# A seven-product block multiplication for the input projection of a streaming encoder layer

## The chip, the cores and the metric

The kernel runs on one core of a Trainium2 chip. A core has a matrix engine, TensorE (PE in the profile, with its weight loads as PEld), and three engines for elementwise work: VectorE (DVE), ScalarE (ACT) and GpSimd (POOL). SyncE (SP) issues the transfers between HBM and the on-chip memory SBUF; matmul results land in PSUM. The metric is the device time in microseconds.

## The reference

One layer of an encoder is computed for 2048 prompt tokens and 64 sample tokens, all in float32. The input is row-normalised and multiplied by one wide matrix, and the columns of the product feed two branches:

```python
h = rmsnorm(x, norm_g) @ w_in                     # (tokens, 1024) @ (1024, 6144)
qa, ka, va, za, qb, kb, vb, zb, ga, gb = jnp.split(h, _split_points(), axis=-1)
```

Branch A is differential attention (q and k row-normalised per 64 columns, a chunk mask, the difference of two softmaxes, times v); the sample also attends to 4096 cached keys. Branch B is chunkwise retention with a running state. Each branch is normalised, gated by silu(z) and projected; sigmoid gates merge the two, and a last projection with a residual gives y. The outputs are y, the new k and v, and the retention states.

## The kernel before

Every float32 product that needs precision is made of three matmuls in the format that the profile calls fp32r: an operand is cast (high part), the cast is subtracted from the original (low part), and high x high, high x low and low x high are summed in PSUM.

The input projection runs over two halves of the tokens. `w_load` brings W in pieces of 256 KB, `w_piece` casts each on ACT (L470), and `w_low` subtracts on POOL (L480; three early pieces on DVE, L477). This is done for both halves, 192 pieces in all. `mm_group` (L516) goes through the eight 128-row slices of the inner dimension and issues a trio of matmuls for each. For v, k, q and the retention's v the tokens are stationary and 512 or 256 columns of W move (`natural`; the output lies with tokens on partitions). For the rest W is stationary and 512, 320 or 256 tokens move (`transposed`). The rows of x are normalised and turned by PE transposes (`x_tile`, L385); q and k are normalised with a row sum (L680) and turned as well (L707). `opening` orders the first token tile by hand.

All results go to scratch tensors in DRAM. A second stream of work, `z_stream`, reads them back for attention (`qk_block`, `softmax`, `at_pv`), the cached sample attention and the retention blocks; the third, `out_stream`, makes the two branch projections (`m_tile`, L1685 to L1687) and the output projection (`y_tile`, L1758 to L1760).

The order on PE, ACT and DVE is fixed when the program is built: each stream is a generator, and a planner, `loop`, always advances the most urgent one whose operands and buffers are ready by its own estimate of durations. On the chip each engine then takes its instructions strictly in that order, and waits where something is late. Buffers are counted by name in `BUFS`: "mm" are the PSUM banks of the projection, "w" the split pieces of W. DMAs are all issued by SP, in order.

## Time and profile before

| | |
|---|---|
| runs | median 1970.54 us of 3 (1969.14 to 1971.57) |
| profiled execution, span | 1970.5 us |
| granted PE clock, mean | 0.998 |
| busy: PE, DVE, ACT, POOL | 99%, 53%, 50%, 21% |
| projection matmuls at L516, three groups each of 1280 and 824 | 1363 us and 765 us busy |
| DMA | 286 MB, 145 GB/s on average |

A row of groups names line, engine, operation, output and inputs with their shapes, the count, then the busy time, the mean duration of one in ns and the idle time before it with what ended it. Matmuls overlap in the pipeline, so the busy times of L516 add up to more than the span; for PE the distance between the starts of two matmuls says what one costs. In a row of waits stand the total, the number of times and the longest, in us. A row of the timeline begins with start and duration in us; a row on one line gives the shortest, median and longest duration in ns.

### The profile page before, as it was taken

To read this page: it belongs to the slowest core of one execution; us is meant where nothing else is said; L and a number is where in the kernel's file an instruction comes from. 1 tells how busy PE (TensorE), PEld (TensorE's weight loads), DVE (VectorE), ACT (ScalarE), POOL (GpSimd) and SP (SyncE) were. 2 spreads that over 40 slices of the span, in tenths; PEclk is the share of its full clock that TensorE was granted. 3 is DMA by queue.
4 is the path that set the end of the run, shared out by engine and by line. 5 is a ranking of instruction groups with operands and counts; after the bars stand their busy time and mean duration, and the time that the engine had idled before them with its cause. 6 is when DMAs were issued, how large, how long until landed. Compare 5 with 4: busy or idle time off the path is not lost. (4 is left out here: it accounts for less than half of the span.)

```text
span 1970.5 us, 34013 instructions
## 1 busy us (share of the span) xinstructions
PE 1954.8 (99%) x12158; PEld 1753.9 (89%) x12158; DVE 1048.8 (53%) x2795; ACT 993.2 (50%) x2190; POOL 418.9 (21%) x387
## 2 busy tenths in 40 slices
PE   9999999999999999999999999999999999999999
PEld 7878999999988989999998888888888888888997
DVE  6553665536555236547757656635753356444433
ACT  6432776655544436436756666635654554333321
POOL 2310211212111121212112112112112434222210
PEclk9999999999999999999999999999999999999999
DMA  7647554336655656664352342553234666444432
GB/s 245 212 129 195 152 158 122 110 89 164 180 162 166 163 158 194 189 198 148 105 144 92 97 134 78 160 148 97 65 94 130 197 215 205 145 134 136 140 94 60
DMA packets 332429, 286.03 MB, mean 145 GB/s; under 512 B 65250, under 2 KB 296930, under 8 KB 332259
## 3 DMA queue, kind: packets, MB, share of 16 engines
q1 hardware_dynamic: 332258, 283.85, 49.0%
q8 instruction: 96, 1.57, 0.4%
q14 instruction: 75, 0.61, 0.1%
HBM read 187.22 MB, written 91.49 MB: 141 GB/s over the span
## 5 line engine op out<-in xcount | busy, mean ns | idle before, releaser
L516 PE MATMUL mm<-xh,wh 128*128 128x512 f32 (+2 forms) x1280 | 459.1, 359 | 0.0
L516 PE MATMUL mm<-xh,wl 128*128 128x512 f32 (+2 forms) x1280 | 452.3, 353 | 0.0
L516 PE MATMUL mm<-xl,wh 128*128 128x512 f32 (+2 forms) x1280 | 451.7, 353 | 0.0
L480 POOL TENSOR_TENSOR wl<-ws,wh 128x512 fp32r<-128x512 f32 x189 | 257.0, 1372 | 814.9 <-ACT wh L470 629.5
L516 PEld LDWEIGHTS mm<-xh,wl 128*128 128x128 f32 x1280 | 241.0, 188 | 31.6
L516 PEld LDWEIGHTS mm<-xh,wh 128*128 128x128 f32 x1280 | 241.3, 189 | 29.0 <-issue 0.2
L516 PEld LDWEIGHTS mm<-xl,wh 128*128 128x128 f32 x1280 | 241.6, 189 | 27.9
L516 PE MATMUL mm<-wh,xh 128*128 128x256 f32 (+1 forms) x824 | 258.4, 314 | 1.2 <-DVE tlo L753 1.0
L516 PE MATMUL mm<-wh,xl 128*128 128x256 f32 (+1 forms) x824 | 253.4, 308 | 0.0
L516 PE MATMUL mm<-wl,xh 128*128 128x256 f32 (+1 forms) x824 | 253.1, 307 | 0.1
L1119 DVE TENSOR_TENSOR atl<-at,ath 128x512 fp32r<-128x512 f32 (+1 forms) x144 | 93.8, 660 | 162.6 <-ACT ath L1117 162.6
L810 ACT COPY ev<-mm 128x512 f32<-128x512 f32 x140 | 71.5, 511 | 194.1 <-PE mm L516 166.0
L516 PEld LDWEIGHTS mm<-wh,xh 128*128 128x128 f32 x824 | 156.7, 190 | 10.9 <-DVE tlo L753 1.4
L516 PEld LDWEIGHTS mm<-wl,xh 128*128 128x128 f32 x824 | 156.9, 190 | 9.2 <-POOL wl L480 0.3
L516 PEld LDWEIGHTS mm<-wh,xl 128*128 128x128 f32 x824 | 156.7, 190 | 8.0
L1035 ACT ACTIVATE row<-row,a_mx 128x1024 f32<-128x1024 f32 (+7 forms) x160 | 153.9, 963 | 12.9 <-DVE a_mx L1015 12.6
L1005 DVE CUSTOM_DVE_ANT_0 row<-s,dfar 128x512 f32<-128x512 f32 (+2 forms) x192 | 118.6, 631 | 54.5 <-PE s L997 54.0
L470 ACT CAST wh<-ws 128x512 fp32r<-128x512 f32 x192 | 116.2, 619 | 44.8 <-PE mm L516 18.5
L1117 ACT CAST ath<-at 128x512 fp32r<-128x512 f32 (+1 forms) x144 | 79.0, 564 | 104.8 <-PE at L1104 97.4
L996 PE MATMUL s<-K,q 128*128 128x512 f32 (+3 forms) x320 | 118.7, 374 | 1.4 <-DVE a_acc L1005 1.4
L997 PE MATMUL s<-K,q 128*128 128x512 f32 (+3 forms) x320 | 115.2, 363 | 0.4 <-DMA q<-qT 0.4
L1057 DVE SCALAR_TENSOR_TENSOR row<-row,a_w 128x1024 f32<-128x1024 f32 (+4 forms) x96 | 103.6, 1086 | 14.4 <-ACT row L1054 14.1
(238 smaller groups left out, 4036.1 us busy)
## 6 DMA issues: line engine op xcount, KB each, us to landing
ws<-in_w_in_dram SPq DMA_DIRECT2D x192, 256.0 KB, 3.0
q<-qT SPq DMA_DIRECT2D x128, 128.0 KB, 3.1
V<-vN SPq DMA_DIRECT2D x24, 512.0 KB, 5.5
K<-kT SPq DMA_DIRECT2D x48, 256.0 KB, 4.2
gt<-gaT SPq DMA_DIRECT2D x64, 132.0 KB, 2.1
gt<-gbT SPq DMA_DIRECT2D x64, 132.0 KB, 2.2
xt<-in_x_prompt_dram SPq DMA_DIRECT2D x16, 512.0 KB, 6.1
kn<-in_cache_k_T_dram SPq DMA_DIRECT2D x32, 256.0 KB, 3.7
```

What stands on the lines that cost most here:

```text
L470: self.nc.scalar.copy(h, st)
L480: self.nc.gpsimd.tensor_sub(l, st, h.bitcast(F32))
L516: nc.tensor.matmul(ps, p, q, start=c == 0 and i == 0, stop=c == KC - 1 and i == 2)
L810: nc.scalar.copy(ev, ps)
L996: nc.tensor.matmul(ps, q1s, kk, start=True, stop=False)
L997: nc.tensor.matmul(ps, q2s, kk, start=False, stop=True)
L1005: nc.vector.tensor_tensor_reduce(out=units[k0 // 1024][:, k0 % 1024:k0 % 1024 + n], in0=ps, in1=tab, scale=-SLOPES[h], scalar=3.0e38, op0= ...
L1035: nc.scalar.activation(u, u, AF.Exp, bias=mx, scale=-1.0, accum_out=lp[:, k:k + 1])
L1057: nc.vector.scalar_tensor_tensor(out=u0, in0=u0, scalar=w[:, 0:1], in1=u1, op0=ALU.mult, op1=ALU.add)
L1117: nc.scalar.copy(ah[:, :w], at[:, :w])
L1119: nc.vector.tensor_sub(al[:, :w], at[:, :w], ah[:, :w].bitcast(F32))
```

## The change

The tokens of each of three groups (two, three and three 256-token pairs; the first with the sample) are split into two halves of 288 or 384, the inner dimension into two halves of 512, and W into 24 blocks of 256 columns, each of two halves of 128. For such a 2x2 by 2x2 block product the usual eight block products become seven, P1 to P7 (Winograd's form of Strassen's scheme): four combinations of the x blocks, made once per group, four of the W blocks, made for every block and group, and sums of the products. In each product a W block (or combination) is stationary and 288 or 384 tokens move.

`x_half` normalises x (now read already turned, in a layout prepared by the host) and forms the combinations; those of later groups are stored to DRAM and fetched back (`x_fill`). `w_comp` forms the combinations of W (T1 to T4 in the wr buffers) and splits all seven into high and low parts (wc). Two helpers, `tt` and `cast`, place each of these operations on POOL or on DVE or ACT by the planner's clock. `proj` issues the products in the order P1, P6, P2, P5, P7, then P1 of the next block, P3, P4, three PSUM banks in turn; `evac` copies or adds the results. Everything now leaves the projection with channels on partitions, so v, k and the retention's v are turned by PE afterwards (`turned`, L1716; L894), while the transposes of x and q fall away, and the q and k norms use a matmul with a block-ones matrix (L1776). V is fetched per pair of key tiles, the pools of the output stage open when the projection's close, and attention runs over three token groups instead of two halves.

```diff
-ROWS = 10
-BUFS = {"thi": 1, "tlo": 2, "ev": 3, "q": 2, "K": 4, "V": 4, "ath": 2, "atl": 2,
-        "ws": 3, "w": 12, "r_o": 1, "r_sq": 1, "r_y": 1, "r_hi": 1, "r_lo": 1, "state": 2,
-        "mm": 2, "s": 2, "at": 2, "pv": 1, "tp": 1,
+ROWS = 9
+BUFS = {"ev": 5, "t5": 6, "q": 2, "K": 4, "V": 3, "ath": 2, "atl": 2, "wc": 5, "wr": 7, "state": 1, "xs": 4,
+        "mm": 3, "s": 2, "at": 2, "pv": 1,
         "oz": 11, "og": 16, "gt": 8, "wst": 4, "m": 16, "xt": 2, "yt": 2}
 LAT = 250.0
...
+GROUPS = [(0, 2, 32), (2, 3, 0), (5, 3, 0)]
+
+ORDER = ["P1", "P6", "P2", "P5", "P7", "P3", "P4"]
+NCP = 24
...
-    def mm_group(self, ps, n, us, wsl, x, wfirst, last, between=None):
-        nc = self.nc
-        seg, xsl = x
-        if ps.shape[0] == 64:
-            both = self.both
...
-            ops = ((a, xh), (a, xl), (b, xh)) if wfirst else ((xh, a), (xh, b), (xl, a))
...
-            for i, (p, q) in enumerate(ops):
-                nc.tensor.matmul(ps, p, q, start=c == 0 and i == 0, stop=c == KC - 1 and i == 2)
-                self.P(n)
...
+    def tt(self, op, out, a, b, n, ready, pool=None):
+
+        if pool is None:
+            pool = max(self.pool, ready) + 2.6 * n < max(self.dve, ready) + 1.25 * n + (BIAS[max(0, self.turned_w) // NCP] if self.xcount[0] == 2 else 0.0)
+        eng = self.nc.gpsimd if pool else self.nc.vector
+        getattr(eng, "tensor_" + op)(out, a, b)
+        return (self.G if pool else self.V)(n, ready)
+
+    def cast(self, out, a, n, ready):
+        if max(self.pool, ready) + 1.35 * n + 50 < max(self.act, ready) + 0.84 * n + 165 + CBIAS:
+            self.nc.gpsimd.tensor_copy(out, a)
+            self.pool = max(self.pool, ready) + 1.35 * n + 50
+            return self.pool + LAT
+        self.nc.scalar.copy(out, a)
+        return self.A(n, ready)
...
+    def x_half(self, g, u, got, rx, pre):
...
+        a21, t21 = yield from self.x_stage(g, u, 1, 0, "K")
+        a22, t22 = yield from self.x_stage(g, u, 1, 1, "K")
+        t21 = yield from norm(1, 0, a21, t21)
+        t22 = yield from norm(1, 1, a22, t22)
+        ts1 = self.tt("add", s1, a21, a22, 2 * n, t22)
+        ts3 = self.tt("sub", a21, a11, a21, 2 * n, ts1)
+        t = max(t11, ts1, ts3)
+        if t > self.pe:
+            yield t - LAT
+        ts2 = self.tt("sub", a11, s1, a11, 2 * n, t)
+        t = max(t12, ts2)
+        if t > self.pe:
+            yield t - LAT
+        ts4 = self.tt("sub", a12, a12, a11, 2 * n, t)
+        for j, x, t in ((1, a11, ts4), (3, s1, ts2), (4, a21, ts3), (5, a12, ts4), (6, a22, ts1)):
+            self.give("K" if j in (4, 6) else "row", (yield from split(j, x, t)))
...
+    def w_comp(self):
+        nc = self.nc
+        for n in range(3 * NCP):
+            yield lambda: len(self.wq) > 0 and len(self.wq[0]) == 5
+            (b11, t11), (b12, t12), (b21, t21), (b22, t22), (b3, _) = self.wq.pop(0)
+
+            def split(k, r, t, last=True):
+                yield from self.take("wc")
+                w = self.sb(self.wp, [128, 2, 4, 128], "wc", dt=F32R)
+                if t > self.pe:
+                    yield t - LAT
+                t = self.cast(w[:, 0], r, 512, t)
+                yield t
+                t = self.tt("sub", w[:, 1], r, w[:, 0].bitcast(F32), 512, t)
+                self.wch[n, k] = (w, t)
+                if last:
+                    self.give("wr", t)
+                return t
+
+            t1 = yield from split("P1", b11, t11, False)
+            self.turned_w = n
+            yield max(t12, t1 - LAT)
+            t1 = self.tt("sub", b11, b12, b11, 512, t1)
+            yield t22
+            t2 = self.tt("sub", b3, b22, b11, 512, t1)
+            t3 = self.tt("sub", b12, b22, b12, 512, t1)
+            yield from split("P6", b3, t2, False)
+            t4 = yield from split("P2", b21, t21, False)
+            t4 = max(t4, t2)
+            yield t4 - LAT
+            t4 = self.tt("sub", b21, b21, b3, 512, t4)
+            self.give("wr", t4)
+            for k, w, t in (("P5", b11, t2), ("P7", b12, t3), ("P3", b22, t22), ("P4", b21, t4)):
+                yield from split(k, w, t)
+
+    def proj(self):
+        seq = []
+        for n in range(3 * NCP):
+            first, last = n % NCP == 0, n % NCP == NCP - 1
+            seq += [(n, "P1")] if first else []
+            seq += [(n, "P6"), (n, "P2"), (n, "P5"), (n, "P7")]
+            seq += [] if last else [(n + 1, "P1")]
+            seq += [(n, "P3"), (n, "P4")]
+        bank = {"P1": "a", "P6": "a", "P7": "a", "P4": "a", "P2": "b", "P5": "c", "P3": "c"}
+        after = {"P6": "T", "P7": "U2", "P4": "C22", "P3": "V"}
+        nc = self.nc
+        st = {}
+        for n, k in seq:
+            g, j = n // NCP, ORDER.index(k)
+            nn = cols(g)
+            p0, np_, s = GROUPS[g]
+            if k == "P1":
+                st[n] = {}
+            q = st[n]
+            b = bank[k]
+            if b not in q:
+                yield from self.take("mm")
+                q[b] = self.psum("mm")[:, :nn]
+            fresh = k in ("P1", "P2", "P5")
+            if k in after:
+                yield lambda: after[k] in q
+                if q[after[k]][1] > self.pe:
+                    yield q[after[k]][1]
+            yield lambda: len(self.xr.get((g, j), ())) == 2 and (n, k) in self.wch
+            w, t = self.wch.pop((n, k))
+            t = max(t, *self.xr[g, j])
+            if t > self.pe:
+                yield t
+            x = self.xt[g, j]
+            for c in range(4):
+                wh, wl, xh, xl = w[:, 0, c], w[:, 1, c], x[:, 0, c], x[:, 1, c]
+                for m, (u, v) in enumerate(((wh, xh), (wh, xl), (wl, xh))):
+                    nc.tensor.matmul(q[b], u, v, start=fresh and c == 0 and m == 0,
+                                     stop=c == 3 and m == 2, skip_group_check=True)
+                    t = self.P(nn)
+                if c == 1:
+                    yield self.pe
+            self.give("wc", t)
+            if n % NCP == NCP - 1:
+                self.xfree[g, j] = t
+            self.spawn(self.evac(n, k, q, t), 0, "w")
+            yield self.pe
+
+    def evac(self, n, k, q, t):
+        nc = self.nc
+        nn = cols(n // NCP)
+        if k in ("P1", "P6", "P5", "P4"):
+            yield from self.take("ev")
+            c = self.sb(self.ep, [128, 384], "ev", "ev")[:, :nn]
+            if t > self.pe:
+                yield t
+            nc.scalar.copy(c, q["c" if k == "P5" else "a"])
+            t = self.A(nn, t)
+            q[{"P1": "T", "P6": "U2", "P5": "V", "P4": "C21"}[k]] = (c, t)
+            if k == "P4":
+                self.give("mm", t)
+                self.finish(n, 0, 1, c, t)
+            return
+        b, src, ct, a = {"P2": ("b", "T", 0, 0), "P7": ("a", "V", 1, 1), "P3": ("c", "U2", 1, 0)}[k]
+        yield lambda: src in q
+        c, t2 = q[src]
+        t = max(t, t2)
+        if t > self.pe:
+            yield t
+        nc.vector.tensor_add(c, q[b], c)
+        t = self.V(nn, t)
+        if k == "P7":
+            q["C22"] = (c, t)
+        else:
+            self.give("mm", t)
+        self.finish(n, ct, a, c, t)
+
...
+        yield lambda: self.live["w"] == 0
+        self.z2.close()
+        self.z3 = self.es.enter_context(self.tc.tile_pool(name="p3a", bufs=1))
+        self.ms = self.z3.tile([128, 8, 2, 64], F32R, tag="ms", name="ms")
+        self.ogs = []
+        self.wout = []
+        self.spawn(self.out_prep(), 5)
+        yield lambda: len(self.wo[0]) == 4 and len(self.wo[1]) == 4
+        self.spawn(self.out_stream(), 8)```

The order of the instructions at three places. PE (the matrix engine), from its first real work. Before: the norm weights spread over the partitions (gz), transposes of x, then the projection, one 512-column matmul at a time (xh and xl are the high and low parts of x, wh those of W):

```order
L304 MATMUL s<-gz,ones 128x512 x2
L316 MATMUL at<-ones 128x128 x2
L385 MATMUL tp<-ident,xt 128x128 x4
L385 MATMUL pv<-ident,xt 128x128 x4
L574 MATMUL mm<-wh,xh_114 128x512
L574 MATMUL mm<-wh,xl_115 128x512
```

Now (dg spreads a row norm; x_195, x_299, x_204 and x_303 are the x operands of P1, P6, P2 and P5):

```order
L1628 MATMUL mm<-x_195,wc 128x288 x12
L1411 MATMUL s<-dg,ones 128x128 x2
L1409 MATMUL s<-dg,ones 128x32
L1628 MATMUL mm<-x_299,wc 128x288 x12
L1628 MATMUL mm<-x_204,wc 128x288 x12
L1628 MATMUL mm<-x_303,wc 128x288 x12
```

The transposes are gone, and the second product, P6, reads a combination of all four x blocks. DVE, where that combination is made (xa, xs and xR hold blocks and combinations, two half slices each; x_299 is the operand of P6):

```order
L1476 SCALAR_TENSOR_TENSOR xa<-xa,gT,xR 128x288 x4
L1353 TENSOR_TENSOR xR<-xa 128x576
L1353 TENSOR_TENSOR xa<-xa 128x576
L1353 TENSOR_TENSOR xa<-xR,xa 128x576
L1353 TENSOR_TENSOR x_299<-xa,x_299 128x576
L1353 TENSOR_TENSOR xa<-xa 128x576
L1353 TENSOR_TENSOR x_306<-xa,x_306 128x576
L1353 TENSOR_TENSOR x_313<-xa,x_313 128x576
L1353 TENSOR_TENSOR x_299<-xa,x_299 128x576
```

The second half of P6's operand is split after five other operations of the same kind. Before, DVE did two subtractions per x tile here (L393). POOL, the same stretch (wr are W blocks and combinations, wc their parts):

```order
L1353 TENSOR_TENSOR wc<-wr,wc 128x512
L1353 TENSOR_TENSOR wr<-wr 128x512 x2
L1358 CAST wc<-wr 128x512 x2
L1353 TENSOR_TENSOR wc<-wr,wc 128x512 x2
L1358 CAST x_204<-xa 128x576
L1353 TENSOR_TENSOR wc<-wr,wc 128x512
```

Before, POOL had a single row here, `L480 TENSOR_TENSOR wl<-ws,wh` thirteen times; now combinations, casts and parts of x stand between the parts of W.

At the end of the projection, PE now:

```order
L1628 MATMUL mm<-x_12793,wc 128x384 x6
L872 MATMUL s<-rqk 128x128 x4
L877 MATMUL at<-ident,rqk 128x128 x4
L894 MATMUL at<-ident,rru 128x128 x4
...
L956 MATMUL at<-ident,rru 128x128 x4
L1135 MATMUL mm<-ogh,w_o_diffh_20230 128x264
L1136 MATMUL mm<-ogl,w_o_diffh_20230 128x264
L1137 MATMUL mm<-ogh,w_o_diffl_20231 128x264
```

Between the last projection matmul and the first of the output stage stand only steps of two retention blocks (L872 to L956; the third follows among the first output matmuls). Before, a projection matmul (L516) stood directly ahead of L1685.

1311 lines of the change are left out of this document (562 added, 749 removed).

## The prediction

> **What bounds the kernel now.** I read the page's busy times and slices first, then what TensorE (PE) waited for, then the spacing of its matmuls.
>
> ```profile
> PE 1954.8 (99%) x12158; PEld 1753.9 (89%) x12158; DVE 1048.8 (53%) x2795; ACT 993.2 (50%) x2190; POOL 418.9 (21%) x387
> PE   9999999999999999999999999999999999999999
> POOL 2310211212111121212112112112112434222210
> PEclk9999999999999999999999999999999999999999
> q1 hardware_dynamic: 332258, 283.85, 49.0%
> ```
>
> PE is busy in all 40 slices at full granted clock; DVE and ACT are half idle, POOL four fifths. A busy PE is not a PE at its peak, so the waits come next.
>
> ```profile
> PE mm L574 <- ACT wh L470: 2.0, 2, 1.3
> PE s L996 <- DVE a_acc L1005: 1.4, 2, 0.8
> 17.80 0.48 PE L574 MATMUL mm<-wh,xh 128*128 128x512 f32 x1
> ```
>
> The largest wait of PE on any line is 2.0 us in the whole run; from 17.80 us on, the matmuls follow each other without a gap. So the time is the sum of PE's spacings, and PE work that is taken out comes off the end as long as the helpers deliver. How far apart matmuls of each width start (first and last row of a stretch of one width, from the timeline; a row gives start, duration, instruction):
>
> ```profile
> 1500.22 0.40 PE L516 MATMUL mm<-xl,wh 128*128 128x512 f32 x1
> ...
> 1503.89 0.39 PE L516 MATMUL mm<-xh,wl 128*128 128x512 f32 x1
> ...
> 401.01 0.31 PE L516 MATMUL mm<-xh,wh 128*128 128x320 f32 x1
> ...
> 401.88 0.39 PE L516 MATMUL mm<-xh,wh 128*128 128x512 f32 x1
> ...
> 301.85 0.28 PE L516 MATMUL mm<-xh,wh 128*128 128x256 f32 x1
> ...
> 302.55 0.28 PE L996 MATMUL s<-K,q 128*128 128x256 f32 x1
> ...
> 300.10 0.34 PE L996 MATMUL s<-K,q 128*128 128x384 f32 x1
> 300.28 0.34 PE L997 MATMUL s<-K,q 128*128 128x384 f32 x1
> ...
> 23.23 0.60 PE L385 MATMUL tp<-ident,xt 128*128 128x128 f32 x4
> 23.67 0.60 PE L385 MATMUL pv<-ident,xt 128*128 128x128 f32 x4
> ```
>
> 512 columns: 3.67 us over 16 starts, 0.229 us. 320: 0.87/6, 0.145. 256: 0.70/6, 0.117. 384: 0.18 from one pair, 0.173 on the line between 256 and 512; I take 0.175. 288, between 256 and 320: 0.132. A 128-column transpose: 0.44/4, 0.11.
>
> **The change, part by part.** First PE. The old projection by its forms (each row stands for a trio of equal counts):
>
> ```profile
> L516 PE MATMUL mm<-xh,wh 128*128 128x512 f32 x768 | 304.6, 397 | 0.0
> L516 PE MATMUL mm<-wh,xh 128*128 128x512 f32 x184 | 74.4, 404 | 0.2 <-ACT raw L672 0.2
> L574 PE MATMUL mm<-wh,xh 128*128 128x512 f32 x8 | 4.5, 556 | 2.0 <-ACT wh L470 2.0
> L516 PE MATMUL mm<-wh,xh 128*128 128x256 f32 x640 | 184.0, 288 | 1.0 <-DVE tlo L753 1.0
> L516 PE MATMUL mm<-xh,wh 128*128 128x256 f32 x256 | 73.7, 288 | 0.0
> L516 PE MATMUL mm<-xh,wh 128*128 128x320 f32 x256 | 80.8, 315 | 0.0
> L512 PE MATMUL mm<-wh,xs 128*128 128x512 f32 x24 | 9.4, 394 | 0.0
> L707 PE MATMUL tp<-ident,raw 128*128 128x128 f32 x128 | 19.3, 273 | 0.0
> ```
>
> 3 x 960 x 0.229 = 660 us, 3 x 896 x 0.117 = 314 us, 3 x 256 x 0.145 = 111 us, and some 15 us for the sample's tile (L512 and its sisters): 1100 us. The new one has 24 column blocks x 7 products x 12 matmuls in each of three token groups, 2016 of 288 columns and 4032 of 384: 2016 x 0.132 + 4032 x 0.175 = 266 + 706 = 972 us. **Saved: 128 us.** Transposes: the 136 of x (L385) and 136 of q and k (L707) go, 30 us; 144 of v and k (L1716, L1719) and 68 of the retention's v (L894) come, 23 us; so do 96 matmuls for the q and k norms (L1776, L1777), 15 us, and 18 that spread the row norms, 2 us. **Net +10 us.** The profiled execution's own time is its span, 1970.5 us, and the runs' median is 1970.54, so no correction is needed: with helpers that keep up, 1970.5 - 128 + 10 = 1852 us.
>
> Now the helpers, which is where the price lies. One pass is one column block for one token group; there are 72. Each needs 7 casts, 7 subtractions for low halves and 4 combinations of W, all 128x512: 504 casts and 792 tensor-tensor operations where 192 and 192 stood. The built program puts 669 of the 792 and 189 casts on POOL, 123 on DVE, 315 casts on ACT. Their prices, and what happens when DVE and POOL meet:
>
> ```profile
> L480 POOL TENSOR_TENSOR wl<-ws,wh x189: 1258/1296/2281, 10.2 to 1566.0; 128x512 fp32r<-128x512 f32 x189
> L398 POOL CAST xs<-xl 128x256 fp32r<-128x256 f32 x2 | 0.7, 402 | 0.0
> L470 ACT CAST wh<-ws 128x512 fp32r<-128x512 f32 x192 | 116.2, 619 | 44.8 <-PE mm L516 18.5 <-DMA ws<-in_w_in_dram 11.5 <-issue 9.7
> L1704 DVE TENSOR_TENSOR gt<-mm,gt 128x264 f32<-128x264 f32 x64 | 27.5, 429 | 30.0 <-PE mm L1687 30.0
> L1119 DVE TENSOR_TENSOR atl<-at,ath 128x512 fp32r<-128x512 f32 x112 | 76.2, 690 | 137.6 <-ACT ath L1117 137.6
> L1202 DVE TENSOR_TENSOR atl<-kn,ath x32: 680/693/1773, 443.2 to 629.8; 128x512 fp32r<-128x512 f32 x32
> L477 DVE TENSOR_TENSOR wl<-ws,wh x3: 1394/1759/1762, 13.3 to 16.3; 128x512 fp32r<-128x512 f32 x3
> L1049 DVE TENSOR_TENSOR a_w<-a_w,nlam x64: 159/160/1144, 203.6 to 1454.1; 128x1 f32<-128x1 f32 x64
> 10.19 7.32 POOL L480 TENSOR_TENSOR wl<-ws,wh 128x512 fp32r<-128x512 f32 x5 [8.93 <-ACT wh L470]
> 13.30 4.76 DVE L477 TENSOR_TENSOR wl<-ws,wh 128x512 fp32r<-128x512 f32 x3
> ```
>
> POOL: 1.30 us for a tensor-tensor of 512; 0.40 for a cast of 256, so between 0.5 and 0.8 for one of 512 (I take 0.74). DVE: 0.43 at 264 and 0.69 at 512, some 0.15 us plus 1.05 ns a column. The last five rows are the ones to see. A DVE operation with one operand in PSUM (at) takes 0.69 on average, always. The same operation with both operands in SBUF has a median of 0.69 but reaches 1.77; the three at the start, inside POOL's run of five, took 1.59 each; a one-column multiply goes from 0.16 to 1.14. They wait for the POOL instruction in progress, on average half of one, 0.65 us, when they meet one. POOL pays as well: its five took 7.32 us where five alone take 6.5, and the longest is 2.28. I charge POOL 0.3 to 0.45 us per DVE operation of 512 and in proportion. Today POOL is 21% busy and this hardly shows.
>
> The sum by stages, from the counts of the built order and these prices (PE, DVE, POOL: own work; n: DVE instructions with two tensors in SBUF, and behind it the time that they take from POOL):
>
> - Passes 0 to 5: PE 75, DVE 100, POOL 82 us, n 125 (39 us). The first x group's norm, combinations and seven splits, and the second group's preparation, all lie here, and P6 needs them ahead of everything but P1.
> - Passes 6 to 17: PE 163, DVE 123, POOL 154, n 108 (40).
> - Passes 18 to 35: PE 315, DVE 228, POOL 273, n 209 (56).
> - Passes 36 to 71: PE 846, DVE 647, POOL 635, n 330 (105).
>
> Low bound of a stage: POOL with what DVE takes in the first (82 + 39 = 121 us against 75 and today's start of some 10: 36 lost), and nothing in the others, where POOL's own work fits under PE. High bound: DVE with its waits, T = D + n x 0.65 x POOL/T, or POOL with its losses, whichever is longer. Stage one 146, plus 8 until the first x tile is there: 69 lost. Stage two 189 or 194: 31. Stage three 346 or 329: 31. Stage four 808 or 740 under 846: none. I take about the middle, since five buffers of split W and three PSUM banks carry some of a delay and not all: 50 + 14 + 10 = 74 us.
>
> The seam to the output projection: the pool of the out-projection weights now opens only when the projection's pools close, behind its last store; two retention blocks and part of a third are PE's cover, and they are chains.
>
> ```profile
> wst<-in_w_o_ret_dram SPq DMA_DIRECT2D x16, 128.0 KB, 3.1
> L1628 POOL TENSOR_TENSOR on<-on,z 128x264 f32<-128x264 f32 x64 | 52.2, 822 | 97.0 <-DMA on<-obT 44.5 <-DMA on<-oaT 33.7 <-DVE ms L1723 5.7
> ```
>
> Ahead of the first output matmul lie a store and a load of 3.1 us each, a split, and five steps of the gate chain, one of 0.82 and four nearer 0.43: some 10 us, of which nothing to all is bare, and 15 with the loads queued behind each other. I take 8 of 0 to 15.
>
> At nothing: DMA. W is read 288 times 256 KB instead of 192 (25 MB), x combinations are parked in DRAM and fetched (22 MB), V comes in 144 pieces of 256 KB instead of 24 of 512 (25 MB): 72 MB on 284, and the queue's 49% leaves room. ACT gets 393 more instructions of about 0.5 us, 200 us on 993, and stays below PE or DVE in every stage. If either cover failed, it would add to stages one and two first.
>
> **Sum: 1852 + 74 + 8 = 1934 us**, and from the bounds 1888 to 1998.
>
> **The rivals.** *The helpers keep up.* If operations meet less often than at random, PE's sum stands: 1852 to 1888, say 1865. For it: PE never waited more than 2 us in any place. Against: the first stage, where DVE alone has 100 us of work against 75.
>
> *DVE and POOL exclude each other, and the supply sets the time through two token groups: slower.* If each meeting costs a whole POOL instruction, as at L477 (+0.9 us), the three stages become 156, 196 and 364 us: 79 + 33 + 49 = 161 lost, with the seam 2023; I put this rival at 2000. It decides from 118 us of loss on. For it: the L477 rows, and evacuations queue behind waiting operations on DVE, while the next product needs their bank. Against: L1202's median of 0.69, though POOL works on W in its stretch too.
>
> The Trainium skill (SBUF — State Buffer, section "Who interferes with whom") says that a Vector instruction with two SBUF inputs and a GpSimd instruction that reads SBUF lock each other out for the whole instruction. The L1119 and L1202 rows agree with it; by that rule this rival is the expected case, and its 2023 us would stand.
>
> *The weight load bounds narrow matmuls, and the change saves nothing:* 6048 loads at 0.188 us,
>
> ```profile
> L516 PEld LDWEIGHTS mm<-xh,wl 128*128 128x128 f32 x1280 | 241.0, 188 | 31.6
> ```
>
> would be 1137 us, 165 more than 972: 2017. The 256-column trios start every 0.117 us with such loads, so they overlap; hardly possible. The Trainium skill (Perfetto Trace Analysis, "Identifying the Most-Contended Engine") would judge PE's headroom by LDWEIGHTS busy time; the spacing of the 256-column rows shows here that it is not the limit.
>
> **How the numbers follow.** Forecast (36 to 114 us lost in all, 1888 to 1966) 0.56; helpers keep up 0.14; exclusion 0.22; between the two, within 0.2% of today, 0.06; weight load 0.02. This kernel's runs lie within 0.12%, so 0.2% (1966.6 to 1974.5) is about what can be told from no change. Faster 0.70, same 0.06, slower 0.24. Forecast 1934 us. The range of 1872 to 2000 leaves about one in ten at each end: below, most of the first rival's cases; above, half of the second's. Faster cases alone: 1865 to 1966.
>
> **What would show it.** Right: starts of L1628 0.132 and 0.175 us apart once running; PE half idle in the first 150 us, waiting for L1353 on DVE or POOL, and the seventh pass beginning at about 130 to 155 us; the 512-wide L1353 on DVE at 1.1 us or more on average while L1660 (PSUM operand) stays at 0.45 to 0.55; PE over 97% busy from about 700 us on; under 15 us idle before L1135. Wrong: PE idle that goes on through passes 36 to 71, a wider spacing of L1628, or a first stage that ends before 110 us.

## The result, and the profile after

The changed kernel takes 2160.24 us (median of four runs, 2158.05 to 2162.5) against 1970.69 us (the kernel before with one run more than above): 1.096 times as long, with an interval of 1.0947 to 1.0978. It is slower by 190 us, where 36 us fewer were forecast (1934, range 1872 to 2000).

The page of the kernel after: busy times and two of the rows of slices.

```profile
PE 1927.6 (89%) x11856; PEld 1805.2 (84%) x11856; DVE 1497.2 (69%) x3200; ACT 1158.6 (54%) x2583; POOL 1365.4 (63%) x1141
...
PE   3776888898998999999999899999999958999999
...
PEclk5888899999999999999999999999999978999999
```

PE was busy in all forty slices before; now it is below nine tenths in thirteen of them, and half idle near the end. No helper has taken its place: DVE is at 69%, POOL at 63%, ACT at 54%. The granted clock is lowered in the first eighth and at the dip near slice 33.

The stages of the kernel after, cut where passes 6, 18 and 36 begin (84 projection matmuls to a pass), at the last projection matmul and where the output stage runs (times count from the start of the profiled span; columns: window, its length, busy time of PE, PEld, DVE, ACT and POOL with instructions, granted clock, DMA share, GB/s):

```profile
0.00:188.30 188.30, 106.00 (x595) 97.78 (x596) 140.18 (x250) 83.02 (x200) 114.88 (x91) 0.75 0.64 204
188.30:405.30 217.00, 183.34 (x1214) 169.99 (x1214) 160.12 (x282) 119.77 (x301) 161.71 (x116) 0.94 0.68 190
405.30:780.80 375.50, 342.05 (x2130) 324.01 (x2128) 291.54 (x557) 224.30 (x541) 308.80 (x242) 0.97 0.67 189
780.80:1723.30 942.50, 891.76 (x5456) 854.05 (x5454) 694.58 (x1550) 562.99 (x1138) 659.34 (x553) 0.98 0.60 166
1723.30:1800.00 76.70, 50.42 (x307) 45.16 (x307) 50.18 (x114) 54.59 (x122) 25.64 (x29) 0.78 0.63 193
1800.00:2160.70 360.70, 354.05 (x2166) 314.23 (x2164) 160.56 (x449) 113.96 (x285) 95.03 (x113) 1.00 0.44 132
```

Read each row as length less PE busy (idle), and PE busy times one less the clock (what the lower clock can have cost at most, since it is also low while PE idles). PE's work itself is busy time times clock.

| stage | PE idle | lowered clock, at most | predicted loss |
|---|---|---|---|
| passes 0 to 5 | 82.3 | 27 | 50 (36 to 69), behind a start of some 10 |
| passes 6 to 17 | 33.7 | 11 | 14 (0 to 31) |
| passes 18 to 35 | 33.5 | 10 | 10 (0 to 31) |
| passes 36 to 71 | 50.7 | 18 | 0 |
| seam | 26.3 | 11 | 8 (0 to 15) |
| output stage | 6.6 | 0 | 0 |
| sum | 233 | 77 | |

Before, idle was 15.7 us (1970.5 less 1954.8) and the clock cost at most 4 us (0.998). With the clock at its bound, the 190 us are 217 more idle and 73 for the clock, less about 100 of PE work saved. An estimate from the matmuls that start at about twice their usual distance puts the clock nearer 50 us and the work saved nearer 115. Some 255 us are then waiting, since the windows count each matmul as busy up to its modelled end and the distances do not.

What PE waited for, in place of the 2.0 us that was the longest entry before: the four longest entries of its waits (total, times, longest), then the two entries for split W:

```profile
PE mm L1628 <- ACT ev L1647: 42.7, 16, 11.0
PE mm L1628 <- DVE ev L1660: 19.9, 9, 11.1
PE s L1411 <- DVE dg L1406: 18.1, 8, 7.5
PE at L1777 <- POOL qlo L1353: 17.2, 13, 5.3
...
PE mm L1628 <- DVE wc L1353: 3.7, 1, 3.7
...
PE mm L1628 <- POOL wc L1353: 0.2, 1, 0.2
```

The first two are evacuations of a product's bank: short operations, 0.45 and 0.52 us, that stand behind other work. On ACT this work was mostly the row statistics of x, attention, and the casts and norms of q and k; on DVE it was mostly work on x and on W. For a part of W that was not split yet, the matmuls waited 3.9 us in all. Added up over all entries of this view, DVE ended 120 us of PE's waits, ACT 75, POOL 21 and DMA 11; 88 us stood ahead of projection matmuls and 139 ahead of others (attention, norms, retention, output). And the helpers' own groups, whose idle time (behind the bar, with what ended it) says whom they waited for:

```profile
L1353 POOL TENSOR_TENSOR wc<-wr,wc 128x512 fp32r<-128x512 f32 x440 | 618.2, 1412 | 153.2 <-ACT wc L1361 131.2 <-DMA vsN<-raw 2.7 <-DVE row L490 2.6
L1361 ACT CAST wc<-wr 128x512 fp32r<-128x512 f32 x315 | 191.5, 620 | 185.8 <-PE mm L1628 95.3 <-POOL wr L1353 83.5 <-issue 2.9
L1358 POOL CAST wc<-wr 128x512 fp32r<-128x512 f32 x189 | 135.6, 719 | 183.5 <-PE mm L1628 177.6 <-DVE wr L1353 2.1 <-issue 1.8
L1353 DVE TENSOR_TENSOR wr<-wr 128x512 f32<-128x512 f32 x59 | 49.9, 846 | 77.1 <-POOL wr L1353 71.6 <-DMA V<-vN 3.4 <-DMA q<-qT 1.2
```

The helpers form a ring. POOL waits 131 us for ACT's casts; ACT waits 84 us for POOL's combinations and 95 us for PE to free a buffer; POOL's own casts wait 178 us for PE to free a buffer; DVE waits 72 us for POOL. A wait for a buffer means that the helper was ahead by all the buffers there are, so not every link of the ring holds PE up. No helper is full, and each waits for others. That is a reading of one trace so far; the runs below test parts of it.

### The profile page after: what moved, and what is told of

It is laid out like the page before. It is cut to its first block, busy times and chain, and to the rows that moved or that the text cites. A ratio compares the mean times of both kernels' runs of the same rounds, so it can differ in the third digit from the quotient of the medians.

```text
span 2160.7 us, 36460 instructions
## 1 busy us (share of the span) xinstructions
PE 1927.6 (89%) x11856; PEld 1805.2 (84%) x11856; DVE 1497.2 (69%) x3200; ACT 1158.6 (54%) x2583; POOL 1365.4 (63%) x1141
## 2 busy tenths in 40 slices
PE   3776888898998999999999899999999958999999
## 4 chain that ended last, share of the span: by engine, by line
PE 54%; DVE 10%; POOL 9%; DMA 5%; issue 4%; ACT 3%; SPq 1%; POOLq 0%; DVEq 0%; ACTq 0%
PE mm L1628 23%; POOL wc L1353 4%; PE at L1209 3%; POOL wr L1353 3%; PE at L1211 3%; PE at L1210 3%; PE s L429 2%; PE at L541 2%; PE s L430 2%; PE pv L520 1%; PE s L1137 1%; PE mm L1135 1%; PE mm L1136 1%; PE mm L1137 1%; PE s L1136 1%
## 5 line engine op out<-in xcount | busy, mean ns | idle before, releaser
L1628 PE MATMUL mm<-x,wc 128*128 128x384 f32 (+1 forms) x6048 | 1099.0, 332 | 88.2 <-ACT ev L1647 42.7
L1628 PEld LDWEIGHTS mm<-x,wc 128*128 128x128 f32 x6048 | 1007.6, 195 | 112.6 <-ACT ev L1647 41.9
L1353 POOL TENSOR_TENSOR wc<-wr,wc 128x512 fp32r<-128x512 f32 x440 | 618.2, 1412 | 153.2 <-ACT wc L1361 131.2
L1353 POOL TENSOR_TENSOR wr<-wr 128x512 f32<-128x512 f32 x229 | 338.0, 1479 | 52.7 <-DVE wc L1353 18.2
L1361 ACT CAST wc<-wr 128x512 fp32r<-128x512 f32 x315 | 191.5, 620 | 185.8 <-PE mm L1628 95.3
L1358 POOL CAST wc<-wr 128x512 fp32r<-128x512 f32 x189 | 135.6, 719 | 183.5 <-PE mm L1628 177.6
L1647 ACT COPY ev<-mm 128x384 f32<-128x384 f32 (+1 forms) x288 | 128.7, 447 | 85.3 <-PE mm L1628 65.7
L468 ACT ACTIVATE row<-row,a_mx 128x1024 f32<-128x1024 f32 (+6 forms) x160 | 154.1, 964 | 2.6 <-DVE a_mx L448 2.5
L1660 DVE TENSOR_TENSOR ev<-mm,ev 128x384 f32<-128x384 f32 (+1 forms) x216 | 111.2, 515 | 50.9 <-PE mm L1628 47.3
L429 PE MATMUL s<-K,q 128*128 128x512 f32 (+3 forms) x320 | 123.0, 387 | 17.7 <-DVE a_acc L438 14.9
L490 DVE SCALAR_TENSOR_TENSOR row<-row,a_w 128x1024 f32<-128x1024 f32 (+4 forms) x96 | 126.2, 1324 | 7.7 <-ACT row L487 7.7
L1353 DVE TENSOR_TENSOR wr<-wr 128x512 f32<-128x512 f32 x59 | 49.9, 846 | 77.1 <-POOL wr L1353 71.6
L1209 PE MATMUL at<-woh,mh 128*128 128x512 f32 x256 | 101.7, 397 | 0.6
```

The costliest lines, as they stand in the source:

```text
L429: nc.tensor.matmul(ps, q1s, kk, start=True, stop=False)
L468: nc.scalar.activation(u, u, AF.Exp, bias=mx, scale=-1.0, accum_out=lp[:, k:k + 1])
L490: nc.vector.scalar_tensor_tensor(out=u0, in0=u0, scalar=w[:, 0:1], in1=u1, op0=ALU.mult, op1=ALU.add)
L1209: nc.tensor.matmul(ps, h, wh[:, nsl], start=ct == 0, stop=False)
L1353: getattr(eng, "tensor_" + op)(out, a, b)
L1358: self.nc.gpsimd.tensor_copy(out, a)
```

## The experiments

All are single runs, compared with 2160.24 us. In each, the rules at L1350 and L1357 that choose between DVE, POOL and ACT from the planner's times are replaced by a list of the choices that the changed kernel makes, so that an operation stays on its engine unless the edit moves it. Three ideas stood beside the prediction's own: that DVE and POOL shut each other out (the prediction's second rival), that x of the later token groups is prepared too early (D in the expectations), and, formed after the first runs, that one chain sets the pace: the first x group (G), or POOL's wait for ACT's casts (H). The expectations call the shared port A, POOL's own length B, DVE's queue C and the turn-round of a PSUM bank F. They count times inside a run from the trace's own zero, 11 us ahead of the span: their 199 us for the start of the seventh pass is the 188.3 us here.

### First set: one part changed, the order left to the planner

**All 792 tensor-tensor operations of W on POOL** (keys "l" are low halves, "T" combinations of W, "X" those of x; here and in the next run the edit lies in the list and is shown as what it does):

```diff
-        pool = fixed(key)
+        pool = fixed(key) or key[:1] in ("l", "T")
```

> All 792 two-operand instructions on W go to POOL (before: 669 POOL, 123 DVE); every other placement as in the changed kernel. Theory A (shared port): each of the 123 costs the port 1.29 us instead of 0.69, 81 of them in the first three stages: +49 us, and something in the fourth: 2200 to 2240. Theory C (the evacuations that PE waits for are late because they stand behind W work in DVE's queue): DVE loses 109 us of W work and its waits, so faster, 2080 to 2140.

Measured: 2252.89 us, 93 more.

**The combinations of W on DVE** (229 leave POOL):

```diff
-        pool = fixed(key)
+        pool = fixed(key) and key[:1] != "T"
```

> All 288 combinations of W go to DVE (before: 229 on POOL, 59 on DVE); every other placement as in the changed kernel. Theory A (shared port): 0.60 us less of the port for each of 229, 112 of them in the first three stages: -67 us there, and up to 25 in the fourth: 2070 to 2110. Theory C (evacuations late behind W work in DVE's queue): DVE gets 158 us more in front of the evacuations, so slower, 2200 to 2260.

Measured: 2251.41 us, 91 more. The projection ended earlier, at 1689 us against 1723, and then the seam ran dry. A late window of this run:

```profile
1700.00:1950.00 250.00, 174.30 (x925) 147.37 (x926) 135.24 (x339) 155.12 (x292) 53.32 (x64) 0.78 0.44 134
```

76 us of 250 idle: work that had lain under the projection was left for the end.

**The low halves of W left out** (PE reads the high half in their place):

```diff
-                t = self.tt("sub", w[:, 1], r, w[:, 0].bitcast(F32), 512, t)
...
-                wh, wl, xh, xl = w[:, 0, c], w[:, 1, c], x[:, 0, c], x[:, 1, c]
+                wh, wl, xh, xl = w[:, 0, c], w[:, 0, c], x[:, 0, c], x[:, 1, c]
```

> Leaves out the low halves of W altogether (504 subtractions less, 440 on POOL and 64 on DVE; the products with the low half read the high half instead). The PE work stays. Theory A and B: the helpers' sums fall to 128, 110 and 227 us in the first three stages, so only the first is above PE's 75, 163 and 315; 1900 to 1970. If the losses come from chains and the order written by the planner and not from the amount of W work (theory D), the time stays over 2080.

Measured: 2085.19 us, 75 less.

**x of the second and third token group held back** until the seventh and thirteenth pass:

```diff
+            yield lambda: self.turned_w >= 6 * g
```

> The row norms and the x combinations of the second and third token group start when the 7th and the 13th pass of W work begin, and not as soon as the first group's x is ready; placements on engines as in the changed kernel. Theory D (PE waits because what it needs stands in the in-order queues of DVE, ACT and POOL behind work that is not due yet): the first stage loses that work, the seventh pass begins at 140 to 165 us and not at 199, and the whole takes 2110 to 2145. Theory A (the port's sum): the same work is only done later, within 15 us of 2160.

Measured: 2330.66 us, 170 more. The seventh pass did begin at 144.8 us in place of 188.3, as D said; the time was lost again later. A late window of this run, with 85 us of PE idle:

```profile
1700.00:1950.00 250.00, 165.13 (x945) 139.15 (x943) 162.74 (x429) 188.41 (x346) 48.98 (x57) 0.80 0.49 141
```

**Two gentler forms of the same thought.** The planner told longer times for these operations, 240 columns' worth on DVE and a tenth on POOL:

```diff
-        return (self.G if pool else self.V)(n, ready)
+        return self.G(1.1 * n, ready) if pool else self.V(n + 240, ready)
```

> The planner reckons with longer times for what meets at the port: 0.25 us more for each two-operand DVE instruction on W, x and q, k (0.94 us for 512 columns, as measured on average), 10% more for POOL's. Placements stay; only the order changes. Theory D (order): PE's queue gets other work ahead of late products where there is some, 2090 to 2145. Theories A and F: the work and the turn-round are the same, within 20 us of 2160.

And the norm multiplies of x held while DVE's planned time runs over 300 ns ahead of PE's:

```diff
+                while self.dve > self.pe + 300:
+                    yield self.dve - 300
```

> A norm multiply of x is put into DVE's queue only once the planner's DVE is at most 0.3 us ahead, so that evacuations come between the four or eight multiplies that now stand together. Theory D (order): the waits of up to 11 us for L1660 and L1647 in the first 200 us shrink to about 3, the seventh pass begins 10 to 30 us earlier, 2125 to 2150. Theory A: no change in work, within 10 us of 2160.

Measured: 2212.44 and 2201.43 us, 52 and 41 more (in the second the seventh pass began at 180.3).

**The 144 copies of partial sums on ACT left out** (P2 and P3 add an x tile instead):

```diff
-        if k in ("P1", "P6", "P5", "P4"):
+        if k in ("P1", "P6"):
+            return
+        if k in ("P5", "P4"):
```

> Leaves out the copies of the first and the second partial sum out of PSUM (144 of ACT's 288 copies at L1647), so that P6 and P7 go on accumulating without waiting for them; the two adds that used the copies add an x tile in their place, and instruction counts on PE, DVE and POOL stay. Theory F (three of a pass's seven products accumulate onto a bank that must first be copied out, with one or two products of 1.6 to 2.1 us as slack): the waits on L1647 go, 2050 to 2110. Theory A: ACT's copies don't use the port and its queue gets only 65 us shorter, 2130 to 2160.

Measured: 2195.92 us: 36 *more*, with 144 instructions fewer.

What follows from the set: these runs cannot price a part. The planner writes a new order each time its times change, and a new order alone moves the time by tens of us; work left out made the kernel slower. D is answered in part: starting the later x groups later brings the seventh pass forward by 43 us, but whether the time lost afterwards comes from that or from the new order cannot be told here.

### Second set: the same order on PE

So the planner went on counting each operation as before, and only the instruction behind it was changed. PE's list is then that of the changed kernel, row for row.

**Low halves as memsets**: POOL's 440 subtractions become three memsets each, which read nothing and last longer together, and DVE's 64 become one memset. The low halves of W are then zero.

```diff
+                if fixed(f"l{n}.{k}"):
+                    for _ in range(3):
+                        nc.gpsimd.memset(w[:, 1].bitcast(F32), 0.0)
+                    t = self.G(512, t)
+                else:
+                    nc.vector.memset(w[:, 1].bitcast(F32), 0.0)
+                    t = self.V(512, t)
```

> Leaves out the low halves of W: each of POOL's 440 subtractions for them becomes three memsets of the same 128x512 tile, which read nothing, and each of DVE's 64 becomes one; products and order stay. Theory A (shared port: DVE work with two operands in SBUF and POOL work that reads SBUF cannot run at once, so their own times add up: 176, 207 and 378 us in the first three stages that took 199, 217 and 376): with POOL about as busy but off the port, the time falls by 110 to 230 us, to 1930-2050; the 512-wide L1353 of DVE falls from 0.85-1.0 us to under 0.80 on average and L1476 with it. Theory B (POOL's own length and its in-order queue set the pace, whoever holds the port): within 40 us of 2160 as long as POOL is as busy as before.

Measured: 2065.71 us, 95 less, between the ranges of A and B, with POOL as busy as before:

```profile
PE 1895.1 (92%) x11856; PEld 1789.9 (87%) x11856; DVE 1316.0 (64%) x3200; ACT 1157.5 (56%) x2583; POOL 1359.9 (66%) x2021
```

So not POOL's time makes these 95 us. But the edit drops three things at once: a memset does not contend with DVE, it does not wait for ACT's cast, and DVE's 64 subtractions (63.6 us busy) are 31.0 us of memsets.

**Low halves as copies**: two POOL copies of the uncast block each. They read SBUF, and they don't wait for the cast either.

```diff
-                        nc.gpsimd.memset(w[:, 1].bitcast(F32), 0.0)
+                        nc.gpsimd.tensor_copy(w[:, 1], r)
```

> As the run with memsets, but each of POOL's 440 subtractions for the low halves becomes two copies of the W block (0.61 us each alone), which read SBUF and, like the memsets, don't wait for the cast; the low half is then a second high half. Order as in the changed kernel. Theory A (the port): reads of POOL meet DVE again, so most of the 95 us come back, 2125 to 2170, and the 64 one-column divisions' sums at L478, 0.15 us in the middle with memsets and 0.36 before, go back over 0.25. If the memsets gained by not waiting for the casts: 2050 to 2090, and L478 stays near 0.15 or the time low whatever L478 does.

Measured: 2097.33 us, 63 less, between the two ranges:

```profile
PE 1904.7 (91%) x11856; PEld 1792.9 (86%) x11856; DVE 1380.5 (66%) x3200; ACT 1159.0 (55%) x2583; POOL 1340.0 (64%) x1581
```

**Low halves left out**, in the same order:

```diff
-                t = self.tt("sub", w[:, 1], r, w[:, 0].bitcast(F32), 512, t)
+                t = (self.G if fixed(f"l{n}.{k}") else self.V)(512, t)
...
-                wh, wl, xh, xl = w[:, 0, c], w[:, 1, c], x[:, 0, c], x[:, 1, c]
+                wh, wl, xh, xl = w[:, 0, c], w[:, 0, c], x[:, 0, c], x[:, 1, c]
```

> The W low halves left out as in the second call's first kernel of that kind, but the planner still reckons with them, so that PE's order is that of the changed kernel, row for row; the helpers' queues are the same without these 504 instructions. Against the kernel with memsets in their place (same order, POOL as busy, port free: 2066): if only the port mattered (theory A), 2050 to 2075; if POOL's own length sets part of the pace (theory B), 2040 or less.

Measured: 2037.14 us, 123 less. The three runs are a ladder. From 2160 to 2097, 63 us, POOL's wait for the cast goes, but DVE's busy time also falls by 117 us (1497.2 to 1380.5), so how much of the 63 us is the wait is not shown. From 2097 to 2066, 32 us, the reading goes, at nearly the same POOL busy time (1340.0 and 1359.9) and with 64 us less on DVE. From 2066 to 2037, 28 us, POOL's length goes, with DVE's memsets. The contention shows in an operation that reads two SBUF tensors of one column, and has nothing to do but wait. Groups with smallest, median and longest duration in ns, the kernel after:

```profile
L478 DVE TENSOR_TENSOR a_ls<-a_lp x64: 139/358/1261, 859.9 to 1695.8; 128x1 f32<-128x1 f32 x64
```

With memsets on POOL:

```profile
L478 DVE TENSOR_TENSOR a_ls<-a_lp x64: 90/148/1341, 802.7 to 1595.1; 128x1 f32<-128x1 f32 x64
```

With copies:

```profile
L478 DVE TENSOR_TENSOR a_ls<-a_lp x64: 96/418/1251, 818.5 to 1627.5; 128x1 f32<-128x1 f32 x64
```

With low halves left out:

```profile
L478 DVE TENSOR_TENSOR a_ls<-a_lp x64: 139/150/1259, 790.6 to 1568.4; 128x1 f32<-128x1 f32 x64
```

Median 358 ns beside POOL's subtractions, 418 beside its copies, 148 beside its memsets and 150 with the low halves left out, where POOL still makes casts and combinations. The rival's mechanism is real. The Trainium skill (SBUF — State Buffer, section "Who interferes with whom") says that a GpSimd instruction which only writes SBUF does not disturb a two-input Vector instruction; these rows agree. Its part of the 123 us is about the 32 of the second step at least and can be as much as some 95; the runs do not part it from the wait for the cast and from DVE's own subtractions.

**The combinations of W on DVE, same order**:

```diff
-        eng = self.nc.gpsimd if pool else self.nc.vector
+        eng = self.nc.gpsimd if (pool and key[:1] != "T") else self.nc.vector
```

> The 229 combinations of W that POOL did go to DVE, but the planner reckons as before, so that PE's order is that of the changed kernel, row for row. Theory A (port): 0.60 us less of it for each, 112 of them in the first three stages, 2070 to 2110. Theory C (DVE's queue with the evacuations in it is the limit): 158 us more in it, 2190 or more. The earlier run of this kind (2251) had another order of attention and projection and so can't tell.

Measured: 2169.68 us, 9 more:

```profile
PE 1930.6 (89%) x11856; PEld 1804.1 (83%) x11856; DVE 1589.5 (73%) x3429; ACT 1160.8 (54%) x2583; POOL 1035.2 (48%) x912
```

330 us fewer on POOL, 92 more on DVE, and nothing gained; neither range was met. A rule that had fitted the stages (the time of all that reads SBUF on DVE and POOL, added up) asked for 50 to 90 less and fell.

**POOL's 189 casts of W on ACT**, and **ACT's 315 on POOL**:

```diff
-            self.nc.gpsimd.tensor_copy(out, a)
+            (self.nc.scalar.copy if key[0] == "c" else self.nc.gpsimd.tensor_copy)(out, a)
```

> The 189 casts of W that POOL does go to ACT, order as in the changed kernel. POOL and the port get 189 x 0.61 = 115 us less, ACT 117 us more on 1159. If POOL's one-operand reads hold the port too, at the rate of the low halves (123 us for 568 of POOL and 44 of DVE): 20 to 30 us less, 2130 to 2145. If ACT's queue then holds up the evacuations: 2165 to 2200.

```diff
-        self.nc.scalar.copy(out, a)
+        (self.nc.gpsimd.tensor_copy if key[0] == "c" else self.nc.scalar.copy)(out, a)
```

> The 315 casts of W that ACT does go to POOL, so that a W block is cast and reduced to its low half on one engine; order as in the changed kernel. POOL gets 315 x 0.61 = 192 us more, most of them reads of SBUF, on 1365. Theory H (the hand-overs between ACT and POOL cost most): POOL's 131 us of waits for the cast go, and the time rises by less than 20 us or falls: 2110 to 2180. Theories A and B (port and POOL's length): at the rate of the low halves, (32 + 28) us for 612 us of work, 20 us, and more where POOL reaches its limit in the first 800 us: 2180 to 2260.

Measured: 2172.34 us, 12 more, in the range of a late ACT queue, and 2262.58 us, 102 more, at the upper end of A and B. In the second run the link from POOL's subtraction to ACT's cast is gone (its idle before that group falls from 153 to 30 us), yet the kernel is slower. The group, then the second 200 us of the run:

```profile
L1353 POOL TENSOR_TENSOR wc<-wr,wc 128x512 fp32r<-128x512 f32 x440 | 601.0, 1367 | 30.0
```

```profile
200.00:400.00 200.00, 158.04 (x977) 147.20 (x978) 131.89 (x242) 68.32 (x188) 180.85 (x163) 0.89 0.60 164
```

POOL, with its 315 more casts, is busy 181 of 200 us, PE 158: POOL is the late one there. So H as a single cause falls: a wait that is removed by giving its work to the waiting engine can come back as that engine's length.

**Parts left out.** The norms and combinations of x of the second and third group (x then goes on unmixed and unscaled):

```diff
+        if key[:2] in ("X1", "X2"):
+            return (self.G if pool else self.V)(n, ready)
...
+                if g == 0:
                     nc.vector.scalar_tensor_tensor(out=x[:, k], in0=x[:, k], ...
```

> Leaves out the norm multiplications (32 on DVE) and the combinations (16) of x for the second and third token group; their raw x is stored and fetched in their place, and the order stays. All of this work stands in the first six passes. Theories A and D (port, and helper work queued ahead of what PE waits for): some 18 us of norms, 11 of DVE's and 10 of POOL's combinations and the waits at the port that they cause go, the seventh pass begins at 150 to 170 us, 2110 to 2135. If the first stage is bound by its other chains (loading, casts, norms of q and k), 2145 to 2160.

Measured: 2134.17 us, 26 less, just inside the range of A and D; the seventh pass began at 168.9 us (180 as the expectation counts, later than it asked). The same for the first group alone (`key[:2] == "X0"`, `if g:`):

```diff
+        if key[:2] == "X0":
+            return (self.G if pool else self.V)(n, ready)
```

> Leaves out the norm multiplications (16) and the combinations (8) of the first token group's x; raw x is split in their place, order as in the changed kernel. By the amount of work (theories A and B): 7 us of norms and 6 us of combinations of the port, -10 to -15 us: 2145 to 2150. If the first products wait for a chain through them (theory G: statistics, spread, norm, combination, split), the first product of L1628 starts before 20 us and not at 27, the second pass by 55 and not at 74, and the whole takes 2115 to 2135.

Measured: 2146.86 us, 13 less: about what this much work is worth, and far from what G asked. All 288 combinations of W (products read uncombined blocks):

```diff
+        if key[:1] == "T":
+            return (self.G if pool else self.V)(n, ready)
...
-            yield from split("P6", b3, t2, False)
+            yield from split("P6", b22, t2, False)
```

> Leaves out the 288 combinations of W (229 on POOL, 59 on DVE; the products take the blocks of W as they come), order as in the changed kernel. If the amount of helper work on POOL and the port sets the loss (theories A and B), each is worth what a low half was, (2160 - 2037) / 504 = 0.24 us: 70 us, 2080 to 2105. If the loss lies in chains that the combinations are not part of, over 2130.

Measured: 2069.02 us, 91 less, more than A and B asked. The 144 copies of partial sums, in the same order:

```diff
-            nc.scalar.copy(c, q["c" if k == "P5" else "a"])
+            if k in ("P5", "P4"):
+                nc.scalar.copy(c, q["c" if k == "P5" else "a"])
```

> The 144 copies of the first and second partial sum out of PSUM left out again, this time with the order of the changed kernel on PE, row for row. Theory F (turn-round of the bank that is accumulated onto): the 43 us of waits on L1647 go and some of the late matmuls with them, 2080 to 2120. Theory A: 65 us less for ACT, which is not on the port, 2140 to 2160.

Measured: 2143.89 us, 16 less, in A's range; F falls. With the planner's own new order nearly the same edit gave 36 more: 52 us for the order alone. For the low halves it is 48 (2085 against 2037), for the combinations on DVE 82 (2251 against 2170).

**All of it left out together**: low halves, combinations of W, norms and combinations of x, copies.

```diff
+        if key[:1] in ("T", "X"):
+            return (self.G if pool else self.V)(n, ready)
```

(with the edits of the four runs above)

> Everything that the earlier runs left out one by one is left out together: low halves and combinations of W, norm multiplications and combinations of x of all groups, and the copies of two partial sums; casts, splits of x, norms of q and k and all of PE's work and order stay. If helper work of the change is the cause of nearly all the loss (theories A and B): 1885 to 1930. If the order of the queues and the seam hold 100 us or more of their own (theory D): 1960 to 2010.

Measured: 1974.62 us, 186 less, where the single parts add to 269: they cover each other. That is in the range of the order and the seam (D). Three of its windows:

```profile
0.00:200.00 200.00, 149.11 (x913) 140.33 (x914) 78.39 (x243) 107.00 (x256) 21.79 (x32) 0.91 0.85 271
...
200.00:1500.00 1300.00, 1281.96 (x8256) 1243.91 (x8255) 834.97 (x2184) 812.98 (x1752) 239.61 (x287) 1.00 0.68 191
...
1500.00:1620.00 120.00, 89.82 (x567) 83.68 (x565) 72.22 (x157) 76.72 (x168) 38.12 (x42) 0.86 0.62 188
```

From 200 us to 1500 PE idles 18 us, nearly the full PE of the prediction, so the idle time of stages two to four came from the parts left out. But 51 us of idle in the first 200 us and 30 in the seam stay, with DVE at 39% and POOL at 11% in the first. This kernel, without the added helper work, is still no faster than the one before, and 122 us above the 1852 of PE's sum. In its first 200 us the transfers are at 85%, and ACT waited 15 us for loads of x and 8 for one of W; whether they are the cause of what stays, or the order of the short chains, was not tried.

## Why the prediction was wrong

**PE's saving: right.** Starts of L1628 lie where the prediction put them. Timeline of PE (start, duration, instruction):

```profile
116.25 4.96 PE L1628 MATMUL mm<-x,wc 128*128 128x288 f32 x36
121.04 0.38 PE L1716 MATMUL at<-ident,ev 128*128 128x128 f32 x2
...
901.54 1.22 PE L1628 MATMUL mm<-x,wc 128*128 128x384 f32 x6
902.60 0.39 PE L429 MATMUL s<-K,q 128*128 128x512 f32 x1
```

288 columns: 4.79/36 = 0.133 us (0.132 predicted); 384: 1.06/6 = 0.177 (0.175). The saving of 118 net measures about 100 by the windows and about 115 by the spacings, as estimated above. The rival of the weight load is out by the same rows.

**The bound of a stage: the step that failed.** "DVE with its waits [...] or POOL with its losses, whichever is longer" makes the time of the busier helper the time of the stage. The helpers took no longer than it said. In the first four stages DVE was busy 140, 160, 292 and 695 us, where the prediction had 146, 189, 346 and 808; POOL was busy 115, 162, 309 and 659 us, where it had 121, 194, 329 and 740. But the stages lasted 188, 217, 376 and 943 us, with no helper over 82% of any, and PE idled 82, 34, 33 and 51 us in them. In place of one full helper the traces show queues that run in order and wait for each other, and PE waiting for results of DVE (120 us), ACT (75) and POOL (21).

With the added work left out and PE's order kept, PE is full from 200 to 1500 us, so this work makes the loss of stages two to four, although it fits into the helpers' time. Moving it between helpers gains nothing (9, 12 and 102 us more), leaving it out on any of them gains (123, 91, 26, 16, 13). How much of it acts through hand-overs between queues and how much through the contention of DVE and POOL stays open. Of "five buffers of split W and three PSUM banks carry some of a delay", the first part held for PE (3.9 us of waits for split W) and the second did not (62.6 us for evacuations); no run changed the number of either.

One reading in the sum was off by itself: redone, the prediction's formula gives 182, 338 and 814 us of DVE for stages two to four, not 189, 346 and 808. Stage three then loses 23 us at most and not 31, which takes about 4 us off the forecast and does not change the outcome.

**"Stage four none": wrong**, the largest relative miss, and one of the signs named beforehand (PE idle through passes 36 to 71). Here are 800 to 1600 us, the kernel after and then with low halves left out:

```profile
800.00:1600.00 800.00, 756.45 (x4653) 724.68 (x4653) 595.95 (x1334) 484.81 (x985) 568.71 (x477) 0.98 0.62 172
```

```profile
800.00:1600.00 800.00, 786.08 (x4979) 760.05 (x4978) 564.08 (x1397) 517.10 (x1042) 299.27 (x286) 1.00 0.63 177
```

43.6 us idle become 13.9, though POOL had 29% to spare and DVE 25%.

**Stage one: right in kind, too small.** The seventh pass began at 188.3 us, not at 130 to 155. The x work counted is worth 13 and 26 us by the runs that leave it out; 51 us of idle stay even with all of it out, and beyond a start of some 10 us no term held these.

**The seam: about right ahead of the first output matmul, missing behind it.** The 8 us (0 to 15) were for what lies ahead of the first output matmul. That one starts at 1747.0 us, and PE idles 10.1 us until then; up to 1800 us another 16.2 us are idle, and the clock adds up to 11 over the whole seam. No term held these. The part ahead of that matmul, then the longest waits of PE between 1723.3 and 1800 us:

```profile
1723.30:1747.00 23.70, 13.59 (x86) 12.23 (x85) 15.44 (x34) 19.20 (x44) 8.74 (x11) 0.77 0.59 178
```

```profile
PE at L956 <- DVE rru L950: 8.4, 3, 4.3
PE mm L1135 <- ACT w_o_diffh L1003: 7.6, 1, 7.6
PE at L904 <- ACT rqk L887: 3.1, 1, 3.1
```

The two retention blocks were taken as PE's cover, but they cost 8.4 and 3.1 us of waits themselves. The load and split of the output weights (L1003) held PE up 7.6 us, behind the first output matmul and not ahead of it.

**The clock: missing from the sum.** No term allowed for PE being slower after it has waited. By the two readings above that is some 50 us, and 73 at most, of a miss of 226.

**The exclusion rival: right sign, by a rule that fell too.** Its 2023 us were below the 2160. It takes the busier helper's time for the stage as well, and its first three stages (156, 196 and 364 us) are longer than DVE was busy in them (140, 160 and 292), so that its total came nearer is in part luck. Its mechanism is in the traces, with some 32 to 95 of the low halves' 123 us. The durations moved as it and the prediction said, though less:

```profile
L1353 POOL TENSOR_TENSOR wc<-wr,wc x440: 1254/1296/2929, 14.7 to 1706.6; 128x512 fp32r<-128x512 f32 x147
L1353 DVE TENSOR_TENSOR wc<-wr,wc x64: 675/693/1785, 25.1 to 1325.2; 128x512 fp32r<-128x512 f32 x64
```

On DVE the mean is 1.01 us against the median of 0.69 (1.1 or more was named), and the evacuations from PSUM, L1660, stayed at 0.52.

## What to carry to other kernels

When work is moved from a full engine to helpers that are half idle, their free time is not the measure: no helper here was over 82% of a stage, and the full engine still lost 33 to 82 us in each of four. Ask for each queue whose results now stand behind the added work. A kernel whose bound engine never waits has that from its order, and a part that is added costs the order too; price such a change by leaving parts out while the order is kept, because a planner's new order alone moved this kernel by 48 to 82 us. And give each wait of a clocked engine a second price, for the slower matmuls behind it.

## What was not expected of the hardware

The granted clock falls to half during or just behind waits of a few us, and stays there for a while. PE and DVE at 97 to 109 us in the kernel after (timeline; the bracket is the wait), then the clock in two windows:

```profile
97.10 0.97 PE L1628 MATMUL mm<-x,wc 128*128 128x288 f32 x6
109.13 6.69 PE L1628 MATMUL mm<-x,wc 128*128 128x288 f32 x30 [11.05 <-DVE ev L1660]
115.66 0.38 PE L1716 MATMUL at<-ident,ev 128*128 128x128 f32 x2
```

```profile
98.53 6.29 DVE L1476 SCALAR_TENSOR_TENSOR xa<-xa,gT,xR 128x384 f32<-128x384 f32 x4
104.86 1.91 DVE L1353 TENSOR_TENSOR xR<-xa 128x768 f32<-128x768 f32 x1
106.80 1.90 DVE L1353 TENSOR_TENSOR xa<-xa 128x768 f32<-128x768 f32 x1
108.63 0.81 DVE L1660 TENSOR_TENSOR ev<-mm,ev 128x288 f32<-128x288 f32 x2
```

```profile
97.00:109.00 12.00, 1.07 (x7) 0.84 (x7) 11.90 (x10) 1.97 (x4) 10.22 (x6) 0.66 0.42 164
109.00:113.00 4.00, 3.87 (x16) 3.88 (x17) 3.90 (x7) 2.40 (x6) 3.58 (x3) 0.50 0.01 2
```

An evacuation of 0.4 us stands on DVE behind four multiplies and two combinations for the next x group, which lasted 10.1 us beside a busy POOL; PE waits 11 us; and its next 30 matmuls start 6.53/30 = 0.218 us apart in place of 0.133, a further 2.5 us. In the whole trace the granted clock stands at 0.5 in 29 stretches, 215 us together, each close to a multiple of 3.41 us; before there were 2, with 9 us. The longest, 48 us, lies in the first 57 us. A wait of 1.81 us was enough for one of them:

```profile
629.50 0.44 PE L1777 MATMUL at<-qlo,bones 128*128 128x384 f32 x1 [1.81 <-POOL qlo L1353]
```

```profile
629.90:633.30 3.40, 3.40 (x12) 3.06 (x11) 2.72 (x7) 3.16 (x8) 3.32 (x3) 0.52 0.51 149
```

The Trainium skill (TensorE: Matmul & The Clock Gate, section "Part 1: The HAM clock gate (the "warmup" mystery)") tells of a clock that halves after an idle window of about 3.4 us and comes back after a busy one. The trace agrees in the length of the stretches and in the return; the idle time it needed was shorter.

Where an operation of DVE with two operands in SBUF meets one of POOL that reads SBUF, the later one waits for the other to end. Two of the one-column sums on DVE, then what POOL did at the time:

```profile
859.85 0.96 DVE L478 TENSOR_TENSOR a_ls<-a_lp 128x1 f32<-128x1 f32 x1
860.93 1.25 DVE L478 TENSOR_TENSOR a_ls<-a_lp 128x1 f32<-128x1 f32 x1
```

```profile
859.51 1.29 POOL L1353 TENSOR_TENSOR wc<-wr,wc 128x512 fp32r<-128x512 f32 x1
860.88 1.28 POOL L1353 TENSOR_TENSOR wr<-wr 128x512 f32<-128x512 f32 x1
```

Each sum started inside an instruction of POOL and ended 0.01 to 0.02 us behind it. Of the 64 sums in the kernel after, 35 started with over 0.15 us of a POOL instruction left, casts among them, and all 35 ended within 0.03 us of its end; the other 29 took 0.14 us on average. With memsets on POOL, 27 of 43 such sums ended before POOL's instruction did. It holds the other way round as well: of 84 512-column operations of POOL that started with over 0.15 us of an L1353 operation of DVE left, 83 lasted that rest and 1.10 to 1.18 us more. These operations take 1.30 us in the middle and up to 2.93.
